# A 64-byte gap in on-chip memory ahead of the pools of a decoder trunk's products

## The chip, the cores and the metric

The kernel runs on one core of a Trainium2 chip. The metric is the device time of one execution in microseconds. A core has five engines with a queue each: TensorE (PE; its weight loads are listed apart, as PEld), VectorE (DVE), ScalarE (ACT), GpSimd (POOL) and SyncE (SP), which issues the transfers between the chip's main memory and the core's own memory. The core's own memory has 128 partitions; a tile takes the same range of bytes in each of them, so a tile has one place, counted in bytes from the start of a partition.

## The reference, cut to what matters

Two layers, each of which is a SwiGLU feed-forward block, a mixer and another feed-forward block, with a layer norm behind each. There are 256 tokens and 1024 channels, all in float32.

```python
def swiglu(x, w1, w2):
    g, u = jnp.split(x @ w1, 2, axis=-1)
    return (jax.nn.silu(g) * u) @ w2

def hybrid_mixer(x, w_in, ...):
    proj = x @ w_in
    b_gate, c_gate, v, x_r, y_r, g_logits = jnp.split(proj, SPLITS, axis=-1)
    y_a = (b_gate * causal_depthwise_conv(c_gate * v, sc_w, SHORT_CONV_K)) @ w_out_conv
    xc = causal_depthwise_conv(x_r, rc_w, RNN_CONV_K) + rc_b
    gates = jnp.einsum('bshi,ghij->gbshj', xh, rg_w).reshape(2, bsz, s, D_RNN)
    ...
    y_b = (h * jax.nn.gelu(y_r)) @ w_out_rnn
    g_a, g_b = jnp.split(jax.nn.sigmoid(g_logits + b_merge), 2, axis=-1)
    return (g_a * y_a + g_b * y_b) @ w_o

def reference(x, ...):
    for l in range(DEPTH):
        x = layer_norm(ALPHA * x + 0.5 * swiglu(x, ffn_w1[l, 0], ffn_w2[l, 0]), ...)
        x = layer_norm(ALPHA * x + hybrid_mixer(x, ...), ...)
        x = layer_norm(ALPHA * x + 0.5 * swiglu(x, ffn_w1[l, 1], ffn_w2[l, 1]), ...)
    return x
```

## The kernel before

Each float32 product is made of three matmuls. Every operand is split into a high part, rounded to the type float32r, and a low part, what the rounding left. Products are high by high, low by high and high by low, and the three are summed in PSUM.

The weights come in units of 1 MB, a tile `raw` of 2048 float32 per partition. `emit_unit` loads one (L193, from SP's queue), rounds it into `hi` (L197, ScalarE, or VectorE for the first) and subtracts to get `lo` (L198, VectorE). There are 4 buffers of raw and 6 each of hi and lo. A list of steps holds the program in its order; ahead of each step the units are emitted that are at most six ahead of the units used up. TensorE then does the matmuls in the order of the list.

All matmuls of the products are issued in `mm` (L202): the second argument is the stationary operand, which PE loads as weights ahead of the matmul (128 columns), the third is the moving one. In rows of the profile the moving operand stands first: `gu<-xh,hi` has xh moving and hi stationary. The products come in three shapes.

- With the weights stationary and 256 tokens moving (`mm_cols`): in the feed-forward block the banks `gu`, in the mixer `c`, `v`, `b`, `y`, `ga` and `gb`, with the layer's input xh (high) and xl (low) moving, and `wc` and `wr`, with yh and yl moving. The gates `rg` too, but there the moving operands are `xch` and `xcl`, which are slots.
- With the weights moving, 512 columns wide: `fill`, the first products of a block, with xh and xl stationary, and `acc`, its last product (`form_b`), with hidden values stationary. Those hidden values lie in slots (`h0h`, `h0l`, `hh`, `hl`, `mh`, `ml`) or in yh and yl.
- In the last block half of `acc` is cut into pieces of 256 columns, for the second half of the tokens.

Besides these there are transposes of 128 columns: `xT` of the input, `hT` and `x` of slots, all with the identity `ident`.

The places of the tiles follow from the pools, which lie one after the other. First comes `const`: ident, xtok, xh, xl, yh, yl, gB and bB have sizes that are multiples of 128 bytes and begin at a multiple of 128. Then come the small vectors of L102 to L108, each rounded up to 32 bytes: vec 832, hbm 128, hrg 128, sp2 64, tiny 32, mhalf 32, together 1216 = 9 x 128 + 64. The last of the pool are rows0, rows1 (512 each) and six tiles of 64 bytes, 1408 = 11 x 128. Behind const lie the pools of raw, hi, lo (8192 bytes a tile), the slots (2048 bytes each, 14 of them) and the statistics of the layer norm. So all of raw, hi, lo and the slots begin 64 bytes past a multiple of 128. In the built program ident begins at byte 16512 and the first raw at byte 68800: counted from multiples of 256, xh, xl, yh and yl lie at 128, and raw, hi, lo and the slots at 192.

Of the kernel before, what the change touches and what calls it, by code (L numbers as in the profile page):

```python
# [9 lines left out]
F32 = mybir.dt.float32  # L10
# [4 lines left out]
P = 128  # L15
# [23 lines left out]
def trunk_kernel(  # L39
# [33 lines left out]
    const = ctx.enter_context(tc.tile_pool(name="const", bufs=1))  # L73
# [32 lines left out]
    tiny = const.tile([P, 1], F32, name="tiny")  # L106

    mhalf = const.tile([P, 1], F32, name="mhalf")  # L108

    def load_x(hh):  # L110
        for t in range(NT):
            cols = slice(hh * 512, (hh + 1) * 512)
            nc.sync.dma_start(out=xtok[:, t, cols], in_=x[0, t * P : (t + 1) * P, cols])
# [532 lines left out]
```

## Time and profile before

| | |
|---|---|
| time, three runs | 1224.74, 1224.81, 1225.61 us |
| time of the profiled execution | 1224.83 us |
| its span, first to last instruction | 1223.0 us |
| granted TensorE clock, mean | 0.999 |
| matmuls, and weight loads | 8838 each |
| moved by transfers | 236.30 MB, mean 193 GB/s |

The profile lists an instruction's duration apart from its pace. Matmuls overlap, and a matmul of 256 columns that is listed with 277 ns may be followed by the next after 113 ns. The pace is read from the chain of waits, in which a piece of n matmuls has one length, or from the starts in the timeline.

### The profile page before, as it was taken

Reading aid. Unit: us, or ns where it says so; the run is one execution under the profiler, and the core shown is the slowest. Engines: PE = TensorE matmul, PEld = TensorE weight load, DVE = VectorE, ACT = ScalarE, POOL = GpSimd, SP = SyncE. Lnnn points to the kernel's source line nnn. Section 1 sums busy time; section 2 is a strip of 40 time slices with the busy share of each in tenths; the row PEclk is TensorE's granted clock in tenths of the full one; section 3 lists DMA queues with packets and bytes.
Section 4 is the critical chain, followed back from the end, with each engine's and each line's share of the span. In section 5 each row is a group of like instructions: output and inputs, shape, how many; then the busy total and the mean of one; then the engine's idle time right before and its main releaser. Section 6 shows DMA issues by size and latency. Waiting matters only on the chain.

```text
span 1223.0 us, 20210 instructions
## 1 busy us (share of the span) xinstructions
PE 1207.2 (99%) x8838; PEld 1132.5 (93%) x8838; DVE 825.3 (67%) x794; ACT 591.1 (48%) x572; POOL 14.9 (1%) x20
## 2 busy tenths in 40 slices
PE   7999999999999999999999999999999999999997
PEld 5999988999999889998889998889999998899996
DVE  5766546868997785654575654577699967756533
ACT  5544434576575354443254443265856743544420
POOL 0000000000000000000000000000000000000000
PEclk9999999999999999999999999999999999999999
DMA  9975555638565566565566555565475654755610
GB/s 314 290 228 205 181 198 172 222 121 264 188 203 178 170 224 211 188 205 176 168 223 211 187 206 175 170 224 189 141 250 196 201 179 154 259 185 195 202 40 35
DMA packets 184257, 236.30 MB, mean 193 GB/s; under 512 B 4248, under 2 KB 164200, under 8 KB 184168
## 3 DMA queue, kind: packets, MB, share of 16 engines
q1 hardware_dynamic: 184168, 235.00, 58.6%
q8 instruction: 69, 1.13, 0.4%
q14 instruction: 20, 0.16, 0.0%
HBM read 233.94 MB, written 1.05 MB: 192 GB/s over the span
## 4 chain that ended last, share of the span: by engine, by line
PE 98%; DVE 1%; ACT 0%; DMA 0%; issue 0%; SPq 0%; DVEq 0%; ACTq 0%
PE gu L202 32%; PE acc L202 23%; PE fill L202 11%; PE c L202 4%; PE v L202 4%; PE b L202 4%; PE wr L202 4%; PE gb L202 4%; PE y L202 4%; PE ga L202 4%; PE wc L202 4%; PE rg L202 2%; PE xT L237 1%; DMA raw<-in_ffn_w_dram 0%; PE x L420 0%; PE hT L361 0%
## 5 line engine op out<-in xcount | busy, mean ns | idle before, releaser
L198 DVE TENSOR_TENSOR lo<-raw,hi 128x2048 fp32r<-128x2048 f32 (+1 forms) x218 | 493.8, 2270 | 254.9 <-ACT hi L197 254.6
L197 ACT CAST hi<-raw 128x2048 fp32r<-128x2048 f32 (+1 forms) x216 | 410.1, 1906 | 413.1 <-issue 190.7
L202 PE MATMUL gu<-xh,hi 128*128 128x256 f32 x1152 | 154.8, 277 | 0.0
L202 PE MATMUL gu<-xh,lo 128*128 128x256 f32 x1152 | 154.3, 276 | 0.0
L202 PE MATMUL gu<-xl,hi 128*128 128x256 f32 x1152 | 154.3, 276 | 0.0
L202 PEld LDWEIGHTS gu<-xh,hi 128*128 128x128 f32 x1152 | 141.9, 188 | 0.3
L202 PEld LDWEIGHTS gu<-xl,hi 128*128 128x128 f32 x1152 | 141.6, 188 | 0.0
L202 PEld LDWEIGHTS gu<-xh,lo 128*128 128x128 f32 x1152 | 141.5, 188 | 0.0
L202 PE MATMUL acc<-hi,hl 128*128 128x512 f32 (+1 forms) x180 | 65.8, 366 | 0.0
L202 PE MATMUL acc<-hi,hh 128*128 128x512 f32 (+1 forms) x180 | 65.8, 366 | 0.0
L202 PE MATMUL acc<-lo,hh 128*128 128x512 f32 (+1 forms) x180 | 65.8, 365 | 0.0
L345 DVE TENSOR_TENSOR hv<-hv,gu 128x512 f32<-128x512 f32 x36 | 24.8, 688 | 48.9 <-PE gu L202 48.8
L202 PE MATMUL fill<-hi,xh 128*128 128x512 f32 x192 | 53.7, 403 | 3.4 <-DVE hi L197 2.1
L202 PE MATMUL fill<-hi,xl 128*128 128x512 f32 x192 | 52.8, 398 | 0.6 <-DVE xl L242 0.6
L202 PE MATMUL acc<-hi,yh 128*128 128x512 f32 (+1 forms) x144 | 53.0, 368 | 0.0
L202 PE MATMUL acc<-hi,yl 128*128 128x512 f32 (+1 forms) x144 | 52.9, 368 | 0.0
L202 PE MATMUL fill<-lo,xh 128*128 128x512 f32 x192 | 52.6, 396 | 0.0
L202 PE MATMUL acc<-lo,yh 128*128 128x512 f32 (+1 forms) x144 | 52.4, 364 | 0.0
L202 PEld LDWEIGHTS fill<-hi,xh 128*128 128x128 f32 x192 | 36.0, 192 | 13.3 <-ACT xh L241 4.4
L202 PEld LDWEIGHTS fill<-hi,xl 128*128 128x128 f32 x192 | 36.5, 191 | 9.2 <-DVE xl L242 1.4
L202 PEld LDWEIGHTS fill<-lo,xh 128*128 128x128 f32 x192 | 36.6, 191 | 8.1
L241 ACT CAST xh<-xT 128x512 fp32r<-128x512 f32 x24 | 13.5, 590 | 60.4 <-PE xT L237 60.0
(172 smaller groups left out, 1866.4 us busy)
## 6 DMA issues: line engine op xcount, KB each, us to landing
raw<-in_ffn_w_dram SPq DMA_DIRECT2D x116, 1024.0 KB, 5.1
raw<-in_w_in_dram SPq DMA_DIRECT2D x56, 1024.0 KB, 5.1
raw<-in_ffn_w_dram SPq DMA_DIRECT2D x28, 512.0 KB, 4.1
raw<-in_w_out_conv_dram SPq DMA_DIRECT2D x8, 1024.0 KB, 5.4
raw<-in_w_out_rnn_dram SPq DMA_DIRECT2D x8, 1024.0 KB, 5.3
raw<-in_w_o_dram SPq DMA_DIRECT2D x8, 1024.0 KB, 4.9
raw<-in_rg_w_dram SPq DMA_DIRECT2D x4, 1024.0 KB, 6.6
gB<-in_ln_g_dram SPq DMA_DIRECT2D x6, 512.0 KB, 5.6
```

The source lines that it names most:

```text
L197: (nc.vector.tensor_copy if first else nc.scalar.copy)(hi[:, part], raw[:, part])
L198: nc.vector.tensor_sub(lo[:, part], raw[:, part], f(hi[:, part]))
L202: nc.tensor.matmul(ps, lhs, rhs, start=first, stop=last)
L237: nc.tensor.transpose(ps[:, i * P : (i + 1) * P], xtok[:, t, c * P : (c + 1) * P], ident)
L241: nc.scalar.copy(dh, v)
L345: nc.vector.tensor_mul(o, o, u)
```

## The change

One tile of 16 float32 per partition, 64 bytes, is taken from the pool const behind mhalf. Nothing writes or reads it. What is taken from const later (rows0, rows1 and the six small tiles) and all pools behind const move by 64 bytes. The first raw then begins at byte 68864, which is 269 x 256, and raw, hi, lo and the slots all begin at multiples of 256. ident, xtok, xh, xl, yh, yl, gB, bB and the small vectors stay where they were. The instructions of every engine, and their order, are the same as before.

```diff
@@ -106,6 +106,7 @@
     tiny = const.tile([P, 1], F32, name="tiny")
 
     mhalf = const.tile([P, 1], F32, name="mhalf")
+    const.tile([P, 16], F32, name="gap")
 
     def load_x(hh):
         for t in range(NT):
```

## The prediction

> **What bounds the kernel.** I read the page first, for who is busy and who ends the chain.
>
> ```profile
> span 1223.0 us, 20210 instructions
> PE 1207.2 (99%) x8838; PEld 1132.5 (93%) x8838; DVE 825.3 (67%) x794; ACT 591.1 (48%) x572; POOL 14.9 (1%) x20
> PEclk9999999999999999999999999999999999999999
> PE 98%; DVE 1%; ACT 0%; DMA 0%; issue 0%; SPq 0%; DVEq 0%; ACTq 0%
> ```
>
> TensorE is busy 99% of the span at full granted clock, and 98% of the chain that ended last is PE. So this kernel can only be moved by the pace of its 8838 matmuls, or by the 16 us in which PE is idle. The next view is what the queue of the transfers waits for:
>
> ```profile
> SPq L193 <- DVE lo L198: 922.2, 185, 14.4
> ```
>
> For 922 us the loads of weights wait until a buffer `raw` has been read by the subtraction. Transfers are ahead of the work, not behind it, and VectorE (67%) and ScalarE (48%) have room.
>
> What is left is the pace of the matmuls. No instruction is added, removed or moved by the change; the only thing that differs is where tiles lie. So I look for rows in which the same shape runs at different paces, and ask where its operands lie. In the chain of waits a piece has a start, a length in us, and its count:
>
> ```profile
> 42.09 16.97 PE gu L202 x144
> 59.24 76.20 PE gu L202 x672
> 196.76 11.01 PE fill L202 x48
> 220.63 5.66 PE c L202 x48
> 255.36 2.86 PE rg L202 x24
> 348.16 21.76 PE y L202 x192
> 386.24 21.76 PE wr L202 x192
> ```
>
> gu, c, y, wr and rg are all 128x128 by 256 columns. Yet one takes 76.20 / 672 = 113.4 ns in gu, 21.76 / 192 = 113.3 ns in y and wr, and 2.86 / 24 = 119.2 ns in rg. What differs is the moving operand: in gu, c, y and wr it is xh, xl, yh or yl, which begin at a multiple of 128 bytes, while the stationary one (hi, lo) begins 64 past such a multiple. In rg both are 64 past: the same place within 128 bytes. The last FFN holds the cleaner pair, both out of one loop; of 256 columns, with slots (h0h, h0l) or yh and yl as the stationary operand and hi, lo moving:
>
> ```profile
> 1157.55 0.28 PE L202 MATMUL acc<-hi,h0h 128*128 128x256 f32 x1
> ...
> 1159.95 0.28 PE L202 MATMUL acc<-lo,h0h 128*128 128x256 f32 x1
> ...
> 1185.30 0.28 PE L202 MATMUL acc<-hi,yh 128*128 128x256 f32 x1
> ...
> 1187.91 0.28 PE L202 MATMUL acc<-lo,yh 128*128 128x256 f32 x1
> ```
>
> From the first to the second row lie 20 steps: 2.40 / 20 = 120.0 ns, with both operands 64 past. From the third to the fourth lie 23: 2.61 / 23 = 113.5 ns, with the stationary one on a multiple of 128 and the moving one 64 past. So it is not that hi or lo is off by itself: one operand off is fast, whichever it is; both off is slow.
>
> At 512 columns the relation turns round:
>
> ```profile
> 138.69 0.39 PE L202 MATMUL acc<-hi,h0h 128*128 128x512 f32 x1
> ...
> 140.73 0.39 PE L202 MATMUL acc<-hi,h0h 128*128 128x512 f32 x1
> ...
> 163.86 0.39 PE L202 MATMUL acc<-hi,yh 128*128 128x512 f32 x1
> ...
> 165.92 0.39 PE L202 MATMUL acc<-hi,yh 128*128 128x512 f32 x1
> ```
>
> Nine steps each: 2.04 / 9 = 226.7 ns where both are 64 past, 2.06 / 9 = 228.9 ns where they are 64 apart. If being off were the fault, the first pair would be the slower one here too. The two readings of PE (the moving stream, and the weights of the next matmul that PEld loads beside it) seem to meet, and what counts is how far apart they start. That is my reading of the rows; the trace names no cause. 226.7 is twice 113.3, so I take 113.3 ns per 256 columns as the pace without a meeting.
>
> **The change, part by part.** The tile gap is written and read by nobody; the order of instructions on all engines stays. It moves raw, hi, lo and the slots by 64 bytes, and not xh, xl, yh, yl, xtok or ident.
>
> Matmuls of 256 columns with xh, xl, yh or yl moving: before 64 apart from the weights, after it 0 apart within 128 bytes. How many, by the groups that keep forms apart:
>
> ```profile
> L202 PE MATMUL gu<-xh,hi 128*128 128x256 f32 x1152 | 154.8, 277 | 0.0
> L202 PE MATMUL y<-xh,hi 128*128 128x256 f32 x128 | 17.1, 276 | 0.0
> L202 PE MATMUL rg<-xch,hi 128*128 128x256 f32 x64 | 12.8, 282 | 0.0
> L202 PE MATMUL acc<-hi,yh 128*128 128x256 f32 x32 | 8.8, 276 | 0.0
> L202 PE MATMUL fill<-hi,xh 128*128 128x512 f32 x192 | 53.7, 403 | 3.4 <-DVE hi L197 2.1 <-ACT xh L241 1.3
> ```
>
> Each name has three such rows (high by high, low by high, high by low): gu 3456, and c, v, b, y, ga, gb, wc, wr 384 each, 3072: 6528. The trace shows no pair that is 0 apart and both on a multiple of 128, nor one that is 128 apart within 256, which is what they become (xh lies 128 past a multiple of 256, hi 192 before, 0 after). Bounds from the nearest rows: 120.0 ns, as for the acc pair that is 0 apart; 113.3 ns, as now; and below nothing, 0.87 / 8 = 109 ns, the pace of the transposes:
>
> ```profile
> 18.16 0.87 PE xT L237 x8
> 41.22 0.87 PE hT L361 x8
> ```
>
> They move 128 columns in the time of a weight load. I take 120.0, since that row has the same distance modulo 128, and at both widths distance explains what being off does not. Against it stands the same pair: xT is 0 apart (ident and xtok, both on 128) and hT 64 apart, and they cost the same.
>
> - 6528 less 384 that already run slower (gu 192, with 16.97 / 144 = 117.8 ns, and the first two c of each layer, 192 at 5.66 / 48 = 117.9): 6144 x (120.0 - 113.3) = +41.0 us. With the 119.2 of rg it is +36.
> - Those 384: x (120.0 - 117.9) = +0.8 us.
> - acc of 256 columns with yh, yl: 96 x (120.0 - 113.5) = +0.6 us.
> - Matmuls of 512 columns that are 64 apart now: fill 576 and acc with yh, yl 336: 912 x (226.7 - 228.9) = -2.0 us.
> - rg (192) and acc with slots: 0 apart before and after: 0.
>
> Sum +40.4 us. Nothing hides it: PE is the chain, and a slower PE only gives the other engines more room.
>
> The transfers: raw begins on a multiple of 256 instead of 192 past one. PE waits for them once, at the start:
>
> ```profile
> 2.11 4.66 DMA raw<-in_ffn_w_dram
> ```
>
> ```profile
> raw<-in_ffn_w_dram SPq DMA_DIRECT2D x28, 512.0 KB, 4.1
> ```
>
> The first piece of the chain is 4.66 us; the shortest median landing of such loads on the page is 4.1, so 0.6 us is what it could give, and nothing is the other end. I count 0, as no row compares two places of raw. The Trainium skill, "DMA: Bandwidth & Descriptors", section "How a descriptor splits into AXI transactions", says that a descriptor off a 256-byte boundary is split into more transactions; it speaks of reads. An estimate from that page for 1024 bytes that start 192 past a boundary is 38 beats in place of 32, so about 0.7 us of that piece would go; no run here shows it yet.
>
> The profiled execution took 1224.83 us, 1.8 above its span, and equals the median of 1224.81. So 1224.8 + 40.4 = 1265.2.
>
> **The rivals.**
>
> *Same distance is harmless beyond 128 (no change).* The meeting may repeat every 256 bytes or more. Then 128 apart is as good as 64, the 6528 stay at 113.3, rg and acc keep 120, and only the 512 columns (-2.0 to 0) and the stretches at 117.8 (384 x 4.5 ns = -1.7 to 0, or as much elsewhere) can move: 1221 to 1226, likeliest 1224. For it: rg and acc are 0 apart modulo 256 as well, so the rows can't tell 128 from 256, and xT costs what hT does. The same time comes out if the move does nothing for the matmuls at all. The Trainium skill, "TensorE: Matmul & The Clock Gate", section "Step-by-step: what each phase is for", states that PE has two independent read ports and that loading the next weights takes nothing from the running matmul. By that rule the place would not matter and the sum would be 0; the 119.2 against 113.3 ns of one shape disagrees with it.
>
> *Both off is what costs (a little faster).* On multiples of 128 all would run at the floor: rg 192 x 5.9 = 1.1, acc of 256 with slots, 168 x 6.7 = 1.1, the 512s 2.0, the stretches at 117.8 1.7, together 5.9 us: 1218.9. For it: at 256 columns both-off is the only slow pair. Against: at 512 it is the fast one.
>
> *Every operand that is off costs a step of its own (much faster).* 120.0 with two off, 113.3 with one, 106.7 with none, held up at 109 by the weight load: 6528 x 4.4 = 28.7, with the 5.9 above: 1190. For it: the steps at 256 columns are even. Against: at 512 one off should then be faster than two, and is slower.
>
> **How the numbers follow.** Same distance costs: 0.46. Harmless: 0.27. Both off: 0.17. Every one: 0.10. The first decides where 6144 x its price exceeds the 5.9 us, from 1 ns on. The forecast's own range is 1250 (if the pace becomes 117.8, 6144 x 4.5 = 27.6) to 1270. For 8 in 10 the range must reach over the first three, with the DMA's 0.6: 1217 to 1268; it leaves out the much faster case. About 0.2%, 2.4 us, is what a measurement can tell from no change: faster 0.27, same 0.27, slower 0.46.
>
> **What would show it.** After the change, y and wr rows in the chain at 192 x 120.0 = 23.0 us each instead of 21.76, and the long gu piece at 672 x 120.0 = 80.6 instead of 76.20; rg still 2.86; fill nearer to 48 x 226.7 = 10.9. If y stays at 21.76, the distance doesn't matter modulo 128, and rg tells the rest: 2.72 means both-off, 2.86 means a longer period. y at about 20.9 means that every operand counts. I would be wrong altogether if VectorE's or ScalarE's durations moved enough to make PE wait.

## The result, and the profile after

The changed kernel takes 1262.49 us (median of 4 runs, 1261.28 to 1263.34), the kernel before 1224.94 beside it: 1.0299 times as long, 95% interval 1.0287 to 1.0311. The profiled execution has a span of 1259.5 us, 36.5 more than before.

The page of the changed kernel, its head and the engines' busy time:

```profile
span 1259.5 us, 20210 instructions
PE 1243.6 (99%) x8838; PEld 1166.4 (93%) x8838; DVE 825.8 (66%) x794; ACT 590.2 (47%) x572; POOL 14.9 (1%) x20
```

PE is busy for 36.4 us more with the same 8838 matmuls; VectorE and ScalarE do their work in the time that they took before, 825.3 and 591.1 us. So all of the longer span is pace of matmuls. The chain of waits of the changed kernel, start, length and count of a piece (its lines are numbered one higher):

```profile
35.57 5.76 PE gu L203 x48
42.20 17.08 PE gu L203 x144
59.47 79.76 PE gu L203 x672
200.88 11.17 PE fill L203 x48
225.06 5.70 PE c L203 x48
260.58 2.87 PE rg L203 x24
357.48 22.79 PE y L203 x192
397.34 22.79 PE wr L203 x192
```

y and wr went from 113.3 to 22.79 / 192 = 118.7 ns a matmul, the long piece of gu from 113.4 to 79.76 / 672 = 118.7. rg, whose two operands stayed 0 apart, is where it was. fill went from 229.4 to 11.17 / 48 = 232.7 ns.

In the long pieces the new pace is not the 120.0 of rg; only the first bank of gu in each feed-forward block, behind fill, has that (5.76 / 48 = 120.0). The new pace is also uneven. The view of the tile y, of before and then of after, shows the shortest, median and longest duration of a matmul in ns:

```profile
L202 PE MATMUL y<-xh,hi x128: 276/276/276, 348.0 to 969.2; 128*128 128x256 f32 x128
```

```profile
L203 PE MATMUL y<-xh,hi x128: 279/281/285, 357.3 to 998.1; 128*128 128x256 f32 x128
```

Before, all 128 are alike; after, they spread over 6 ns.

### The profile page after: what moved, and what is told of

It reads as the page before. It is cut to its first block, busy times and chain, and to the rows that moved or that the text cites. A ratio compares the mean times of both kernels' runs of the same rounds, so it can differ in the third digit from the quotient of the medians.

```text
span 1259.5 us, 20210 instructions
## 1 busy us (share of the span) xinstructions
PE 1243.6 (99%) x8838; PEld 1166.4 (93%) x8838; DVE 825.8 (66%) x794; ACT 590.2 (47%) x572; POOL 14.9 (1%) x20
## 4 chain that ended last, share of the span: by engine, by line
PE 98%; DVE 1%; DMA 0%; ACT 0%; issue 0%; SPq 0%; DVEq 0%; ACTq 0%
PE gu L203 33%; PE acc L203 23%; PE fill L203 11%; PE b L203 4%; PE wr L203 4%; PE wc L203 4%; PE v L203 4%; PE y L203 4%; PE ga L203 4%; PE c L203 4%; PE gb L203 4%; PE rg L203 2%; PE xT L238 1%; DMA raw<-in_ffn_w_dram 0%; PE x L421 0%; PE hT L362 0%
## 5 line engine op out<-in xcount | busy, mean ns | idle before, releaser
L203 PE MATMUL gu<-xh,hi 128*128 128x256 f32 x1152 | 160.7, 282 | 0.0
L203 PE MATMUL gu<-xl,hi 128*128 128x256 f32 x1152 | 160.3, 282 | 0.0
L203 PE MATMUL gu<-xh,lo 128*128 128x256 f32 x1152 | 160.2, 282 | 0.0
L203 PEld LDWEIGHTS gu<-xh,hi 128*128 128x128 f32 x1152 | 147.1, 188 | 0.4
L203 PEld LDWEIGHTS gu<-xh,lo 128*128 128x128 f32 x1152 | 146.8, 188 | 0.0
L203 PEld LDWEIGHTS gu<-xl,hi 128*128 128x128 f32 x1152 | 146.8, 188 | 0.0
L203 PEld LDWEIGHTS fill<-hi,xl 128*128 128x128 f32 x192 | 36.5, 191 | 9.9 <-DVE xl L243 1.4
```

Source lines behind the costliest of these rows:

```text
L203: nc.tensor.matmul(ps, lhs, rhs, start=first, stop=last)
```

## The experiments

The theory: PE reads the moving operand of one matmul and the weights of the next at one time, and the distance between the two places, modulo some number of bytes, sets the pace. Rivals: it is the place of raw, hi, lo and the slots by itself (a multiple of 128 or 256, or off one), or the transfers into raw. "Apart" is the place of hi and lo less that of xh, xl, yh and yl, modulo 256: 64 before the change, 128 after.

### All tiles moved by 64 bytes: the distance of before, the places of after

```diff
+    const.tile([P, 16], F32, name="gap")
     ident = const.tile([P, P], F32, name="ident")
```

> The gap stands ahead of ident, so that every tile moves by 64 bytes: raw, hi, lo and the slots begin at multiples of 256 as with the change, and xh, xl, yh, yl move along, to 192 past one; the two operands of each matmul are 64 bytes apart again. If the distance between the operands sets the pace: y at 21.76 us a piece of 192 (113.3 ns), and 1225 us. If the place of raw, hi, lo and the slots does it, or transfers into raw that begin at a multiple of 256: y at 22.79 as with the change, and 1262 us.

Measured: 1224.97 us, ratio 0.9988 (0.9976 to 1.0). The chain of waits of this run:

```profile
59.59 76.20 PE gu L203 x672
348.69 21.76 PE y L203 x192
```

Both pieces have the length of before to the hundredth of a microsecond, though raw, hi, lo and the slots lie where the change put them. Neither their place nor the transfers into raw are what cost.

### xh, xl, yh, yl moved, raw, hi, lo and the slots not: 0 apart

```diff
+    sp2 = const.tile([P, DEPTH, KD], F32, name="sp2")
     ident = const.tile([P, P], F32, name="ident")
 ...
-    sp2 = const.tile([P, DEPTH, KD], F32, name="sp2")
```

> sp2 stands ahead of ident: ident, xtok, xh, xl, yh and yl move by 64 bytes, raw, hi, lo and the slots stay where they were before the change. All operands then lie 192 past a multiple of 256: none on a multiple of 128, and 0 apart. If the distance sets the pace, the matmuls of 256 columns run like rg, at 119.2 to 120.0 ns: y at 22.9 to 23.0 us, fill at 48 x 226.7 ns = 10.9 us, and 1259 to 1265 us. If it is the place of raw, hi, lo and the slots that counts, these are as before: 1225 us.

Measured: 1265.72 us, ratio 1.0324 (1.0307 to 1.0342). Its chain of waits:

```profile
59.85 80.64 PE gu L202 x672
201.64 10.90 PE fill L202 x48
261.16 2.88 PE rg L202 x24
359.08 23.04 PE y L202 x192
```

The tiles that lie between yl and tiny (gB, bB, vec, hbm, hrg) move along too; no matmul reads them. No operand of the products is on a multiple of 128, raw, hi, lo and the slots are where they were, and y, gu and rg all run at 120.0 ns (23.04 / 192, 80.64 / 672, 2.88 / 24), fill at 227.1 (10.90 / 48). These are the paces that the prediction read off the few matmuls that were 0 apart before. The time is half a microsecond from the one predicted for the change.

### A gap of 128 bytes: 64 apart the other way

```diff
-    const.tile([P, 16], F32, name="gap")
+    const.tile([P, 32], F32, name="gap")
```

The minus line is that of the change.

> A gap of 128 bytes in place of 64: raw, hi, lo and the slots begin 64 past a multiple of 256, so that hi lies 64 below xh modulo 256 where it lay 64 above. If only the distance modulo 128 counts, or its size: 1225 us with y at 21.76. If the period is 256 and the sign counts, some other pace of y than 21.76 and than 22.79. If a multiple of 128 is what costs: 1225 us as well.

Measured: 1254.98 us, ratio 1.0238 (1.0215 to 1.026). The chain of waits:

```profile
61.00 79.17 PE gu L203 x672
226.24 5.45 PE c L203 x48
357.59 22.61 PE y L203 x192
```

By its number this is the second case, another pace of y than 21.76 and 22.79: y and gu run at 117.8 ns (22.61 / 192). But that is a pace known from before, where the first gu and c had it with operands 64 apart the usual way. And here the first c of each layer has the faster one, 5.45 / 48 = 113.5. So either the sign counts, or 64 apart has two paces both ways. The runs below take this up.

### The slots alone moved, 64 from hi and lo

```diff
     plo = ctx.enter_context(tc.tile_pool(name="plo", bufs=NBUF))
+    gap = ctx.enter_context(tc.tile_pool(name="gap", bufs=1))
+    gap.tile([P, 16], F32, name="gap")
     act = ctx.enter_context(tc.tile_pool(name="act", bufs=NSLOT))
```

> A gap of 64 bytes between the pools of lo and of the slots, and none in const: the slots alone move, to 64 bytes from hi and lo; xh, xl, yh, yl, hi and lo stay. The matmuls with a slot and hi or lo as their two operands change, and no others. If the distance sets the pace: rg at 24 x 113.3 ns = 2.72 us in place of 2.86 (192 matmuls, -1.1 us in all), acc of 256 columns with slots at 113.3 in place of 120.0 (168, -1.1 us), acc of 512 columns with slots at 228.9 in place of 226.7 (780, +1.7 us); y as before, together 1224.4 us, no change that can be measured. If it is two operands off a multiple of 128 that cost: rg and acc of 256 columns gain the same 2.2 us and acc of 512 loses nothing, 1222.7.

Measured: 1247.45 us, ratio 1.0175 (1.0155 to 1.0195), where both readings expected 1222 to 1225. The chain of waits:

```profile
138.33 57.37 PE acc L204 x246
259.73 2.83 PE rg L204 x24
355.84 22.61 PE y L204 x192
471.45 96.11 PE gu L204 x816
...
659.60 92.50 PE gu L204 x816
```

The matmuls with slots went the way that the distance says, but not all by the expected amount. acc of 256 columns did: 23 steps lie between the next two rows, 2.61 / 23 = 113.5 ns in place of 120.0.

```profile
1183.64 0.28 PE L204 MATMUL acc<-hi,h0h 128*128 128x256 f32 x1
...
1186.25 0.28 PE L204 MATMUL acc<-lo,h0h 128*128 128x256 f32 x1
```

rg went to 2.83 / 24 = 117.9 ns instead of 113.3, and acc of 512 columns the other way, to 233.3 with slots, 57.37 us a piece instead of the 55.97 of this row of the kernel before:

```profile
135.44 55.97 PE acc L202 x246
```

What broke the expectation are products whose operands had not moved. In that piece acc with yh and yl, too, starts every 233.3 ns in place of 228.9. y runs at 117.8 ns, and two pieces of gu out of the same code, in two blocks, at 96.11 / 816 = 117.8 and 92.50 / 816 = 113.4. One distance, two paces, in one execution.

### vps later: does a pace last until something comes between?

```diff
-        if i == 16:
+        if i == 24:
             vectors_pe()
             vectors_post()
```

> The kernel before, with the transposes vps (and the vector work behind them) issued after twelve banks of gu in the first block, not after four. In the kernel before, gu ran at 117.8 ns ahead of vps and at 113.4 behind it. If a pace of operands 64 apart lasts until another kind of matmul comes between (history): 12 x 48 = 576 matmuls at 117.8, less the first 48 perhaps, and the rest at 113.4; the change of pace moves with vps to about 104 us, and the time is 384 x 4.5 ns = 1.7 us longer, 1226.5. If the change of pace comes from something else at that time (clock, transfers, the load of the other engines): it stays at 59 us.

Measured: 1226.09 us, ratio 1.0001 (0.9986 to 1.0015). The chain of waits of the first block:

```profile
41.75 62.19 PE gu L202 x528
103.94 0.18 PE vps L134 x2
104.12 33.94 PE gu L202 x288
```

In the kernel before, gu changed from 117.8 to 113.4 ns at 59 us, right behind vps. With vps moved it doesn't change there: all 528 ahead of vps run at 62.19 / 528 = 117.8. Behind vps it stays at 33.94 / 288 = 117.8, against the expectation. So the pace does last, here over 816 matmuls, and what comes between may change it, and need not. What had changed it at 59 us in the kernel before is not shown. The eight executions of this run fall in two groups, 1224.4 to 1225.3 and 1226.9 to 1228.0 us, and the median lies between them, so that it came near 1226.5 is luck; the profiled one (1227.41) is of the upper group. The nine of the kernel before beside it fall in two as well, 1224.6 to 1225.4 and 1228.3 to 1228.4. By an estimate, 672 matmuls at 117.8 in place of 113.4 cost 3.0 us, so in some of its executions the kernel before, too, may run its first block without the change. None of those was profiled.

### Transposes in between, with 64 apart both ways

In each feed-forward block a transpose into a bank that nobody reads, four times. First with the gap of 128 bytes:

```diff
+        def kick():
+            nc.tensor.transpose(bank("kick")[:, :104], ident[:104, :], ident[:104, :104])
+
         for j in range(NFILL, NPF):
+            if j in (4, 6, 8, 10):
+                step(kick)
             step(lambda j=j: pe(j, 0, ga[j]), None, 1, [ga[j]])
```

> The gap of 128 bytes, which ran gu at 117.8 ns throughout, and in each feed-forward block one transpose of 104 columns into a bank that nobody reads, ahead of the 5th, 9th, 13th and 17th bank of gu. If 64 apart has two paces and history picks: some of the pieces between the transposes run at 113.3 ns, others at 117.8; the places of the tiles are those of the run without the transposes. If 64 below has a pace of its own: all pieces stay at 117.8, and the time is that of the gap of 128, 1255.

Measured: 1256.36 us, ratio 1.0246 (1.0197 to 1.0295). The chain of waits in a later block:

```profile
472.09 16.96 PE gu L203 x144
489.06 0.09 PE kick L381
489.15 21.79 PE gu L203 x192
510.94 0.09 PE kick L381
511.03 22.64 PE gu L203 x192
```

117.8, then 21.79 / 192 = 113.5, then 117.9 ns, with every tile in its place. So 64 below has the faster pace too, and most of the time does not fall into it.

The same edit on the kernel before (64 above):

> The kernel before, with the same four transposes of 104 columns in each feed-forward block, into banks that nobody reads; no tile that a product uses lies elsewhere. If 64 apart has two paces and what runs between picks: some pieces of gu at 117.8 where all ran at 113.4, up to 15 us in all for 3456 matmuls at 4.5 ns. If 64 above is always the faster one: gu stays at 113.4, and the time within 1.5 us (16 transposes of 0.09 us) of that of before.

Measured: 1233.14 us against 1228.28 of the kernel before beside it, ratio 1.0042 (1.0018 to 1.0067). The chain of waits:

```profile
463.52 16.35 PE gu L202 x144
479.86 0.09 PE kick L380
479.95 22.64 PE gu L202 x192
...
525.41 21.81 PE gu L202 x192
```

113.5 ns, then 117.9 behind one transpose, and 113.6 behind a later one. In its profiled execution the kernel before runs nearly all of its gu at the faster of two paces that its layout allows. Here the rows of gu in the chain add up to 400.5 us against 392.7 there: 16 transposes, 1.4 us of work, cost more by switching the pace than by their own time. The medians differ by less, 4.9 us; the nine executions of the kernel before beside this run lie between 1224 and 1234 us.

### Distances that are no multiple of 64

Gaps of 32 and of 96 bytes (8 and 24 elements in the line of the change), which put hi and lo 96 above xh, and 96 below.

> A gap of 32 bytes: raw, hi, lo and the slots at 224 past a multiple of 256, 96 above xh. If only 0 and 64 matter modulo 128: a pace between 113.3 and 120.0 ns for y. If the pace falls with the distance up to 128 (120.0 at 0, 113.3 or 117.8 at 64, 118.7 at 128), something between 113.3 and 118.7. If two places with a common multiple of 64 are needed for an even pace, an uneven one.

> A gap of 96 bytes: raw, hi, lo and the slots at 32 past a multiple of 256, 96 below xh. The same three cases as with 32; if the sign does not count, the paces are those of the gap of 32.

Measured: 1259.02 us (ratio 1.0268, 1.0231 to 1.0304) and 1271.1 us (1.0366, 1.0329 to 1.0403). The chain of waits, 96 above and then 96 below:

```profile
357.41 22.53 PE y L203 x192
...
472.74 96.84 PE gu L203 x816
```

```profile
360.34 23.04 PE y L203 x192
...
477.22 97.91 PE gu L203 x816
```

117.3 and 118.7 ns above, 120.0 below: the sign does count here, and the pace doesn't fall evenly with distance. The 120.0 lies at the very end of what the first case of the expectation allows and outside the second. The third fits both runs, as the durations of y<-xh,hi are uneven (277 to 282 ns, and 278 to 286), but so they are at 128 apart. 96 below has the pace of 0 apart in y and gu, and is the slowest kernel of all.

### lo and the slots moved: two distances inside one bank

The kernel in which nothing was apart, with a gap of 64 bytes between the pools of hi and lo.

```diff
     phi = ctx.enter_context(tc.tile_pool(name="phi", bufs=NBUF))
+    gap = ctx.enter_context(tc.tile_pool(name="gap", bufs=1))
+    gap.tile([P, 16], F32, name="gap")
     plo = ctx.enter_context(tc.tile_pool(name="plo", bufs=NBUF))
```

> sp2 stands ahead of ident, as in the run in which no operands were apart (xh, xl, yh, yl, hi at 192 past a multiple of 256), and a gap of 64 bytes between the pools of hi and lo puts lo and the slots at multiples of 256. Inside one bank the weights then change from hi (0 from xh) to lo (64 from xh), and in rg from hi (64 from the slots) to lo (0 from them). If the distance between the two operands that PE reads at one time sets the pace, matmul by matmul: in gu and y eight steps with hi at 120.0 ns (0.96 us), eight with lo at 113.3 or 117.8 (0.91 or 0.94); in rg the other way round. If a bank has one pace, set by history or by where most of it lies: no difference between hi and lo inside a bank.

Measured: 1268.44 us, ratio 1.0319 (1.0234 to 1.0405). The timeline of PE inside a piece of y, where the starts count:

```profile
360.34 1.12 PE L204 MATMUL y<-xl,hi 128*128 128x256 f32 x8
361.30 1.11 PE L204 MATMUL y<-xh,lo 128*128 128x256 f32 x8
362.24 1.12 PE L204 MATMUL y<-xh,hi 128*128 128x256 f32 x8
363.20 1.12 PE L204 MATMUL y<-xl,hi 128*128 128x256 f32 x8
```

Eight steps with hi take 0.96 us, 120.0 ns each; eight with lo 0.94, 117.5. The pace follows the weights' place within one bank, from group to group, while the moving operand, the bank and the block stay the same. In rg the steps are in groups of two and four, too short to tell 118 from 120 by starts that are given to 10 ns. A piece of rg as a whole takes 2.85 us, between the 2.83 of the run in which its two operands were 64 apart and the 2.88 of 0 apart; two thirds of the one and one third of the other make 2.85. So rg agrees by its sum, though not shown step by step.

## Why the prediction was right

- *Where the time is*: right. The whole of the 36.5 us is in PE's pace.
- *What sets the pace*: the distance between the two operands, not being off a multiple of 128. Moving all tiles brought the old lengths of y and the long gu back, moving xh, xl, yh and yl against the rest made the slow ones, and moving lo changed it between groups of one bank. What the distance sets is which paces can come; where it allows two, something else picks. That the two readings of PE get in each other's way is the reading that fits; no run shows the event itself.
- *First term, 6144 x (120.0 - 113.3) = +41.0*: right in sign and place, too large. Measured in the long pieces 118.7 - 113.3 = 5.4 ns, +33 us. The step that failed is the price: 128 apart was taken for 0 apart, by distance modulo 128. It has a pace of its own in the long pieces, uneven and between the two; the 120.0 came only in the first bank of gu of each feed-forward block and in part of acc (third term). With 0 apart in fact, 120.0 came out throughout, and 1265.72 us. No row of the kernel before had 128 apart, so that its price lay this near to that of 0 apart, and the total within 2.7 us, is in part luck.
- *Second, 384 already slow, +0.8*: 144 of gu went from 117.8 to 17.08 / 144 = 118.6 ns, the 48 ahead of them to 120.0, and c from 117.9 to 5.70 / 48 = 118.8, together +0.4.
- *Third, acc of 256 columns with yh, yl, +0.6*: right, about +0.5. The first 24 of them take 2.76 / 23 = 120.0 ns a step (the rows below), the next 24 118.7.

```profile
1221.10 0.29 PE L203 MATMUL acc<-hi,yh 128*128 128x256 f32 x1
...
1223.86 0.28 PE L203 MATMUL acc<-lo,yh 128*128 128x256 f32 x1
```

- *Fourth, 512 columns, -2.0*: wrong sign, from the same step. fill became slower, 229.4 to 232.7 ns, as 128 apart is not 0 apart there either; at 0 apart it ran at 227.1, as the term had it. Added up over all rows of the chain, gu and the eight other products of 256 columns with xh, xl, yh or yl moving take 33.0 us more than before, acc 1.8 and fill 1.6: 36.4 of the 36.5.
- *rg unchanged*: right, 2.86 and 2.87.
- *The rivals*: "harmless beyond 128" fell with y at 22.79; "both off" fell with rg at 2.87 on multiples of 128; "every operand off costs a step" fell with all operands on multiples and y slower, not at 20.9. The Trainium skill, "TensorE: Matmul & The Clock Gate", section "Step-by-step: what each phase is for", calls PE's two read ports independent. Taken, as in the prediction, to mean that the place makes no difference, this doesn't fit the times here: 120.0 against 113.3 ns by the place alone. Whether it is the ports, no run shows.
- *The transfers, counted at 0*: right for the time. The first load was 4.81 us after the change, no shorter than its 4.66 before. The 4.1 that the prediction held against it is the median of loads of 512 KB; the first loads are of 256 KB, whose median in that view is 6.0.

```profile
2.12 4.81 DMA raw<-in_ffn_w_dram
```

- *What the prediction did not see*: the two paces at 64 apart. It had both in its rows (117.8 and 113.4 in gu) and treated the slower as a few stretches that run badly, though its range began at 1250 for a pace of 117.8. It is the other half of what that distance gives; a layout with the same 64 bytes the other way cost 2.4%. Of the 5.4 ns that a matmul in the long pieces lost by the change, 4.5 are the step between these two paces: what the change took away is in the main the faster one, and no long piece at a distance other than 64 ran at 113 in any run.

## What to carry to other kernels

Where PE bounds a kernel of float32r matmuls of 256 columns, take each pair of moving operand and weights that PE reads together, and compare their places modulo 256 early; here gaps of 32 to 128 bytes cost 2.4% to 3.7%. A multiple of 128 for everything is not a goal by itself, and cost 3.0%. Since a pace can last over hundreds of matmuls and change at a step that does no harm itself, read a gain or loss of a few per cent from the length per matmul in the chain of waits before giving an edit the credit.

## What the runs showed of the hardware that was not expected

- Pace of 256 columns by distance: 0 apart 120.0 ns in all long pieces; 64 apart, either way, 113.3 or 117.8; 128 apart 118.7, in the first bank of gu 120.0; 96 above 117.3 or 118.7; 96 below 120.0. No run tells a period of 256 bytes from a longer one. What picks between two paces is open: in these traces one lasts as long as matmuls of one kind follow each other, and a transpose of 0.09 us between them can switch it either way.
- 512 columns have two paces at 64 apart as well. In the run with the slots moved, fill, whose operands had stayed, took 11.21 us for 48 in the first mixer and 11.02 in the block behind it, 233.5 and 229.6 ns.
- The time that packets of q1 took, as a share of 16 engines' span, of before, after, all moved, and the gap of 128:

```profile
q1 hardware_dynamic: 184168, 235.00, 58.6%
```

```profile
q1 hardware_dynamic: 184168, 235.00, 55.5%
```

```profile
q1 hardware_dynamic: 184168, 235.00, 57.4%
```

```profile
q1 hardware_dynamic: 184168, 235.00, 57.0%
```

Times the spans (1223.0, 1259.5, 1223.6 and 1255.3 us) these are 717, 699, 702 and 716 us. With raw on multiples of 256 (the second and third) the packets take 2% less; in the same way the ten other profiled runs give 713 to 717. As PE doesn't wait for transfers, the time shows none of it. The Trainium skill, "DMA: Bandwidth & Descriptors", section "How a descriptor splits into AXI transactions", states its rule for reads, and raw is what transfers write. Carried over to writes it would give this direction, by an estimate from that page 6 beats in 38, 16%; the gain here is far smaller.
